# First feed-forward: 512-column products with added halves, and half of the modulation tiles on GpSimd and ScalarE

## The chip, the core and the metric

The kernel runs on one core of one Trainium2 chip, as one program. The metric is the device time of the program in microseconds (us). A core has five engines with a queue of instructions each, which run side by side and wait for each other by semaphores: TensorE (PE in the rows, PEld for its weight loads), VectorE (DVE), ScalarE (ACT), GpSimd (POOL) and SyncE (SP), which issues most transfers. An engine works through its queue in order.

## What is computed

Two layers of a decoder trunk on 256 positions of 1024 channels. Each layer has a mixer (layer 0: a state-space group beside attention; layer 1: a convolution module) and a gated feed-forward, both in front of a residual addition. Shift, scale and gate of each come from a modulation vector, the product of a condition vector with a large matrix. Cut to what matters here:

```python
def conv_ffn(h, w_up, w_gate, dw_w, dw_b, w_down):
    g = causal_dwconv(h @ w_gate, dw_w, dw_b)            # width 3 along the positions
    return (jax.nn.silu(g) * (h @ w_up)) @ w_down        # hidden width 2816

cs = jax.nn.silu(c)
for layer in range(2):
    mod = cs @ mod_w[layer] + mod_b[layer]               # 1024 x 6144
    sh1, sc1, g1, sh2, sc2, g2 = jnp.split(mod, 6, axis=-1)
    h = modulate(rms_norm(x, norm_g[layer, 0]), sh1, sc1)
    x = x + g1[:, None, :] * mixer(h)
    h = modulate(rms_norm(x, norm_g[layer, 1]), sh2, sc2)
    x = x + g2[:, None, :] * conv_ffn(h, ffn_w_up[layer], ffn_w_gate[layer], ..., ffn_w_down[layer])
return rms_norm(x, final_g)
```

## The kernel before

Everything is kept transposed: channels on the 128 partitions, the 256 positions (`T`) along a row. Weights come from memory in chunks of 128 x 1024 numbers (512 KB), one transfer each, in the fixed order of `chunk_order`, into 14 buffers (`raw0` to `raw9`, and four halves of `ABT0` and `ABT1`).

**Split products.** For accuracy each weight chunk is split in two: ScalarE writes a rounded copy `hi` (tiles `whi`, `whim`), VectorE the rest `lo = raw - hi` (tiles `wlo`, `wlom`). There are six such pairs of tiles, and a pair is free again when TensorE is through with its chunk (`release`). The activations `h` are split in the same way into a high and a low half of a row. A product of a 128 x 128 weight tile is then made of three parts, hi x high, hi x low and lo x high. `tile_mm` does it in three products of 256 columns into one result of 256 columns. `tile_wide` does the two with `hi` as one product of 512 columns, so that the result is two halves that have still to be added, and the third as a product of 256 columns.

**The feed-forward.** `ffn` goes through 44 chunks, gate and up in turn for 22 hidden blocks; the first three are done ahead in `ffn_lead`, so `run_seq` does 41 chunks of eight 128 x 128 tiles each, 328 tile steps. Its zone is called `b-` in layer 0 and `i-` in layer 1. In layer 0 the steps go by `tile_mm`, in layer 1 by `tile_wide`, and `post` has the additions of the halves for layer 1 alone. After each chunk `post` runs on ScalarE and VectorE: for a gate the width-3 convolution (`gate_tail`, tile `ac`), for an up chunk the product with the silu of the gate (tile `uu`) and its split into `hv` (`up_tail`). Then 22 chunks `down` are multiplied with `hv`, 22 steps for each of the 8 blocks of output; the last step of the first block needs the last `hv`.

**Modulation tiles.** 32 chunks `md` of the modulation matrix (four vectors of eight tiles, list `MD`) are mixed into the order of layer 0's feed-forward and eight (`MD1`) into that of layer 1. VectorE works each off in one instruction (`mod_dve`): the chunk times the condition vector `cb`, with its row sum into `modv`. The result of the product (`junk`) isn't used. After the eighth tile of a vector the bias is added.

**What sets the order.** The instructions are recorded in a `Plan`, which puts them in an order of its own for each engine (`arrange`): it goes through them by time as its cost formulas see it and takes the one with the highest rank among those that are ready, where the table `BONUS` adds a number to the rank of each group of instructions. The order is fixed when the kernel is built. All recorded instructions have the same line in the profile, 487 (of `getattr(getattr(self.nc, eng), fn)(*a, **k)`), so rows are told apart by their tiles.

Of the kernel before, what the change touches and what calls it, by code (L numbers as in the profile page):

```python
# [548 lines left out]
class Emit:  # L549
    def __init__(self, ctx, tc, nc, d, order):  # L550
        self.tc, self.nc, self.d, self.order = tc, nc, d, order
        self.pool = ctx.enter_context(tc.tile_pool(name="base", bufs=1))
        self.psp = ctx.enter_context(tc.tile_pool(name="psum", bufs=1, space=bass.MemoryType.PSUM))
        banks = [self.psp.tile([128, 512], F32, name=f"bank{i}") for i in range(8)]
        self.mm, self.aux = banks[:4], banks[4:]
        self.i_mm = self.i_aux = 0
        t = self.pool.tile
        self.raw_free = [t([128, 1024], F32, name=f"raw{i}") for i in range(RAW_BUFS)]
        self.split_free = [(t([128, 1024], F32R, name=f"whi{i}"), t([128, 1024], F32R, name=f"wlo{i}"))
                           for i in range(SPLIT_BUFS)]  # L560
# [89 lines left out]

    def mod_dve(self, c):
        _, l, s, f = c
        col = self.modv[l][:, s * 8 + f:s * 8 + f + 1]
        self.nc.vector.scalar_tensor_tensor(self.junk, self.raw[c], 1.0, self.cb, op0=OP.mult, op1=OP.mult,
                                            accum_out=col)
        self.done(c)
        if f == 7:
            mc = self.modcols(l, s)
            self.nc.vector.tensor_tensor(mc, mc, self.par("modb", l * 48 + s * 8, 8), op=OP.add)

    def low(self, n):
# [1419 lines left out]
```

## Time and profile before

| | us |
|---|---|
| median of 3 runs | 650.72 |
| lowest and highest | 647.98, 651.05 |
| the profiled execution | 652.09 |
| its span, first to last instruction | 650.3 |
| mixer of layer 0 and lead, up to the first step of zone `b-` | 0 to 164.2 |
| 41 chunks gate and up, layer 0 | 164.2 to 281.1 |
| down, layer 0 | 281.1 to 343.7 |
| convolution module, lead of layer 1 | 343.7 to 463.8 |
| 41 chunks gate and up, layer 1 | 463.8 to 579.0 |
| down, layer 1, and the end | 579.0 to 650.3 |

The rows below are of the profiled execution; the two microseconds between it and its span lie ahead of the first instruction and behind the last. A row of the timeline has the start, the duration, the engine, the operation, what it writes and reads, and its shape; consecutive instructions of one kind are merged with their count. A tile `bank` lies in the matmul's result memory (PSUM), all others in the on-chip main memory (SBUF). An instruction's duration overlaps a little with the next one's, so that the time an instruction costs its engine in a dense stretch is the distance from its start to the next start, its step.

### The profile page before, as it was taken

Reading aid. Unit: us, or ns where it says so; the run is one execution under the profiler, and the core shown is the slowest. Engines: PE = TensorE matmul, PEld = TensorE weight load, DVE = VectorE, ACT = ScalarE, POOL = GpSimd, SP = SyncE. Lnnn points to the kernel's source line nnn. Section 1 sums busy time; section 2 is a strip of 40 time slices with the busy share of each in tenths; the row PEclk is TensorE's granted clock in tenths of the full one; section 3 lists DMA queues with packets and bytes.
Section 4 is the critical chain, followed back from the end, with each engine's and each line's share of the span. In section 5 each row is a group of like instructions: output and inputs, shape, how many; then the busy total and the mean of one; then the engine's idle time right before and its main releaser. Section 6 shows DMA issues by size and latency. Waiting matters only on the chain.

```text
span 650.3 us, 13240 instructions
## 1 busy us (share of the span) xinstructions
PE 640.4 (98%) x5128; PEld 562.5 (87%) x5128; DVE 538.8 (83%) x1059; ACT 404.9 (62%) x736; POOL 41.2 (6%) x99
## 2 busy tenths in 40 slices
PE   8999999999999999999999999999999999999995
PEld 5789876899999999998899987568988888888885
DVE  8698996389999999999657999559999998997641
ACT  3479528897966666654446843377687766675431
POOL 4830000000000000000000222000000000000000
PEclk9999999999999999999999999999999999999998
DMA  8996888765489999999662798496476668764001
GB/s 325 405 377 224 291 324 300 316 217 210 134 288 320 325 331 303 338 328 365 195 196 81 245 325 245 154 380 263 135 280 199 201 214 259 217 210 164 1 0 66
DMA packets 45702, 158.50 MB, mean 244 GB/s; under 512 B 5535, under 2 KB 7112, under 8 KB 45640
## 3 DMA queue, kind: packets, MB, share of 16 engines
q1 hardware_dynamic: 43912, 153.84, 67.6%
q0 software_dynamic: 1152, 3.49, 1.9%
q8 instruction: 40, 0.66, 0.4%
q10 hardware_dynamic: 576, 0.33, 0.2%
q14 instruction: 22, 0.18, 0.1%
HBM read 153.10 MB, written 1.06 MB: 237 GB/s over the span
## 4 chain that ended last, share of the span: by engine, by line
PE 88%; DVE 7%; ACT 2%; DMA 1%; issue 1%; DVEq 0%; SPq 0%
PE bank L487 88%; DVE arena L487 4%; DVE wlo L487 1%; DMA raw<-w_in 1%; ACT CA L487 1%; DVE CS L487 1%; DVE U L487 1%; ACT whi L487 0%; ACT ABT L487 0%; DVE gp L487 0%; DVE nm L487 0%; DVE junk L487 0%; DVE h L487 0%; DVEq L2044 0%; DVE nt L487 0%
## 5 line engine op out<-in xcount | busy, mean ns | idle before, releaser
L487 PE MATMUL bank<-h,whi 128*128 128x256 f32 (+2 forms) x960 | 202.3, 303 | 0.2
L487 PEld LDWEIGHTS bank<-h,whi 128*128 128x128 f32 x960 | 152.4, 189 | 8.7 <-issue 1.0
L487 PE MATMUL bank<-h,wlo 128*128 128x256 f32 (+1 forms) x560 | 155.5, 283 | 0.0
L487 PE MATMUL bank<-h,whim 128*128 128x256 f32 (+1 forms) x664 | 149.1, 311 | 0.0
L487 PE MATMUL bank<-h,wlom 128*128 128x256 f32 x416 | 116.4, 281 | 0.0
L487 PEld LDWEIGHTS bank<-h,whim 128*128 128x128 f32 x664 | 108.2, 189 | 7.7
L487 PEld LDWEIGHTS bank<-h,wlo 128*128 128x128 f32 x560 | 104.5, 189 | 1.3 <-DVE CS L487 0.8
L487 DVE TENSOR_TENSOR wlo<-raw,whi 128x1024 fp32r<-128x1024 f32 x69 | 84.1, 1222 | 13.6 <-ACT whi L487 10.4
L487 ACT ACTIVATE whi<-raw 128x1024 fp32r<-128x1024 f32 x69 | 72.5, 1055 | 20.7 <-PE bank L487 13.7
L487 DVE TENSOR_TENSOR wlom<-raw,whim 128x1024 fp32r<-128x1024 f32 x60 | 72.9, 1222 | 10.5 <-ACT whim L487 10.3
L487 PEld LDWEIGHTS bank<-h,wlom 128*128 128x128 f32 x416 | 78.3, 188 | 0.1
L487 ACT ACTIVATE whim<-raw 128x1024 fp32r<-128x1024 f32 x60 | 62.6, 1054 | 22.7 <-PE bank L487 15.8
L487 PE MATMUL bank<-hv,whim 128*128 128x512 f32 (+1 forms) x236 | 67.7, 351 | 0.0
L487 PE MATMUL bank<-hv,whi 128*128 128x512 f32 x160 | 56.3, 393 | 0.0
L487 PE MATMUL bank<-hv,wlom 128*128 128x256 f32 x192 | 53.9, 281 | 0.0
L487 PEld LDWEIGHTS bank<-hv,whim 128*128 128x128 f32 x236 | 41.3, 189 | 6.2
L487 PE MATMUL bank<-hv,wlo 128*128 128x256 f32 x160 | 44.7, 279 | 0.0
L487 DVE SCALAR_TENSOR_TENSOR ac<-g,pp,ac 128x256 f32<-128x256 f32 x88 | 42.2, 482 | 2.5 <-ACT ac L487 0.8
L487 DVE SCALAR_TENSOR_TENSOR x<-bank,modv,x 128x256 f32<-128x256 f32 x54 | 25.6, 481 | 19.7 <-PE bank L487 19.1
L487 ACT ACTIVATE whi<-ABT 128x1024 fp32r<-128x1024 f32 x28 | 29.3, 1054 | 16.3 <-PE bank L487 15.3
L487 ACT ACTIVATE g<-bank 128x256 f32<-128x256 f32 x40 | 15.3, 382 | 36.4 <-PE bank L487 36.3
L487 PEld LDWEIGHTS bank<-hv,wlom 128*128 128x128 f32 x192 | 36.4, 190 | 0.0
(220 smaller groups left out, 1071.6 us busy)
## 6 DMA issues: line engine op xcount, KB each, us to landing
raw<-w_in SPq DMA_DIRECT2D x213, 512.0 KB, 5.3
ABT<-w_in SPq DMA_DIRECT2D x71, 512.0 KB, 4.9
a<-ap POOLq DMA_DIRECT2D x24, 142.0 KB, 5.4
x<-x_in SPq DMA_DIRECT2D x4, 256.0 KB, 4.2
arena<-scr SPq DMA_DIRECT2D x1, 1024.0 KB, 6.0
cb<-c_in SPq DMA_DIRECT2D x2, 512.0 KB, 4.9
kT<-bc_in SPq DMA_DIRECT2D x1, 512.0 KB, 11.4
out<-junk SPq DMA_DIRECT2D x2, 256.0 KB, 2.0
```

The costliest lines, as they stand in the source:

```text
L487: getattr(getattr(self.nc, eng), fn)(*a, **k)
```

## The change

`run_seq` gets `wide=("gate", "up")` in both layers, so layer 0's 328 steps become one product of 512 and one of 256 columns each, instead of three of 256. `post` then adds the two halves in layer 0 too: for a gate ScalarE copies the first half out of the bank (as it did) and VectorE adds the second half of the bank to it; for an up chunk ScalarE copies the second half out (new) and VectorE adds the first (new); the convolution and the product then read that sum from SBUF and no longer from the bank. Modulation tiles are numbered, and every second one goes to `mod_pool`: GpSimd multiplies the chunk by `cb` in place, then ScalarE copies it onto itself with a row sum into `modv`. The other tiles stay on VectorE. The list of numbers `BONUS` is another one throughout.

```diff
+ON_POOL = (1, 0)
...
-BONUS = {'a-evac': 335.5, 'a-gate_tail': -31, 'a-h_u': 30.1, 'a-lead': 1098.9,
...
+BONUS = {'a-evac': 602.1, 'a-gate_tail': 184.4, 'a-h_u': 1.4, 'a-lead': 2.7,
...
+        self.i_mod = 0
...
-                (self.mod_dve if c[0] == "md" else self.split)(c)
+                (self.mod if c[0] == "md" else self.split)(c)
...
+    def mod(self, c):
+        self.i_mod += 1
+        (self.mod_pool if ON_POOL[self.i_mod % len(ON_POOL)] else self.mod_dve)(c)
+        if c[3] == 7:
+            self.mod_bias(*c[1:3])
+
+    def mod_pool(self, c):
+        _, l, s, f = c
+        w = self.raw[c]
+        self.nc.gpsimd.tensor_tensor(w, w, self.cb, op=OP.mult)
+        self.nc.scalar.activation(w, w, AF.Copy, accum_out=self.modv[l][:, s * 8 + f:s * 8 + f + 1])
+        self.done(c)
+
+    def mod_bias(self, l, s):
+        mc = self.modcols(l, s)
+        self.nc.vector.tensor_tensor(mc, mc, self.par("modb", l * 48 + s * 8, 8), op=OP.add)
...
-        if f == 7:
-            mc = self.modcols(l, s)
-            self.nc.vector.tensor_tensor(mc, mc, self.par("modb", l * 48 + s * 8, 8), op=OP.add)
...
             if t == "gate":
                 nc.scalar.activation(g[:, 2:], ps[:, 0:T], AF.Copy)
-                if l == 1:
-                    ps = g[:, 2:]
-                    v.tensor_tensor(ps, psw[:, T:2 * T], ps, op=OP.add)
+                ps = g[:, 2:]
+                v.tensor_tensor(ps, psw[:, T:2 * T], ps, op=OP.add)
                 self.gate_tail(l, i, ps)
             else:
-                if l == 1:
-                    nc.scalar.activation(u, ps[:, T:2 * T], AF.Copy)
-                    v.tensor_tensor(u, ps[:, 0:T], u, op=OP.add)
-                    ps = u
+                nc.scalar.activation(u, ps[:, T:2 * T], AF.Copy)
+                v.tensor_tensor(u, ps[:, 0:T], u, op=OP.add)
+                ps = u
                 nc.scalar.activation(a, a, AF.Silu)
                 v.tensor_tensor(u, ps, a, op=OP.mult)
                 self.up_tail(i)
...
-        self.run_seq(ffn_seq(l)[3:], self.h, post, mids=mids, wide=("gate", "up") if l == 1 else ())
+        self.run_seq(ffn_seq(l)[3:], self.h, post, mids=mids, wide=("gate", "up"))
```

How the queues move is seen in the order of the instructions as built. On VectorE, in the middle of layer 0's gate and up chunks, stands before (`wlo...` is a split, `junk_1648,modv` a modulation tile, `ac` the convolution, `uu` and `hv` the product and its split):

```order
L487 SCALAR_TENSOR_TENSOR junk_1648,modv1_91<-raw3_72,cb_1649 128x1024
L487 SCALAR_TENSOR_TENSOR ac_0_1643<-g0_0_1641,pp_89,ac_0_1643 128x256 x2
L487 TENSOR_TENSOR wlo1_82<-raw9_78,whi1_81 128x1024
L487 TENSOR_TENSOR uu_0_1645<-bank1_62,ac_0_1643 128x256
L487 SCALAR_TENSOR_TENSOR junk_1648,modv1_91<-raw4_73,cb_1649 128x1024
L487 TENSOR_TENSOR hv_1640<-uu_0_1645,hv_1640 128x256
L487 TENSOR_TENSOR wlo2_84<-raw8_77,whi2_83 128x1024
L487 SCALAR_TENSOR_TENSOR junk_1648,modv1_91<-ABT0_87,cb_1649 128x1024
```

and at the like place now (`g0` from a bank is the added half of a gate, `uu` from a bank that of an up chunk):

```order
L488 TENSOR_TENSOR g0_1_1642<-bank2_63,g0_1_1642 128x256
L488 TENSOR_TENSOR wlo2_84<-raw8_77,whi2_83 128x1024
L488 SCALAR_TENSOR_TENSOR ac_1_1644<-g0_1_1642,pp_89,ac_1_1644 128x256 x2
L488 TENSOR_TENSOR uu_1_1646<-bank3_64,uu_1_1646 128x256
L488 TENSOR_TENSOR uu_1_1646<-uu_1_1646,ac_1_1644 128x256
L488 TENSOR_TENSOR wlo1_82<-raw9_78,whi1_81 128x1024
L488 TENSOR_TENSOR hv_1640<-uu_1_1646,hv_1640 128x256
L488 TENSOR_TENSOR wlo0_80<-ABT1_88,whi0_79 128x1024
```

Two additions have come in for each pair of chunks, and fewer modulation tiles stand between: from the first split of zone `b-` to the last `hv` VectorE has 24 of them before and 9 now, with 44 and 43 splits.

On ScalarE, at the same place, stands before (`whi...` is the other half of a split):

```order
L487 ACTIVATE hv_1640<-uu_1_1646 128x256
L487 ACTIVATE g0_0_1641<-bank0_61 128x256
L487 ACTIVATE ac_0_1643<-bank0_61,pp_89 128x256
L487 ACTIVATE whi0_79<-ABT1_88 128x1024
L487 ACTIVATE ac_0_1643<-ac_0_1643 128x256
L487 ACTIVATE whim0_1631<-raw3_72 128x1024
L487 ACTIVATE hv_1640<-uu_0_1645 128x256
```

and now:

```order
L488 ACTIVATE ac_0_1643<-g0_0_1641,pp_89 128x256
L488 ACTIVATE uu_0_1645<-bank1_62 128x256
L488 ACTIVATE whim0_1631<-raw0_69 128x1024
L488 ACTIVATE ac_0_1643<-ac_0_1643 128x256
L488 ACTIVATE hv_1640<-uu_0_1645 128x256
L488 ACTIVATE g0_1_1642<-bank2_63 128x256
L488 ACTIVATE whim1_1633<-ABT0_87 128x1024
L488 ACTIVATE raw7_76,modv1_91<-raw7_76 128x1024
L488 ACTIVATE uu_1_1646<-bank3_64 128x256
```

The copy of an up chunk's half and the row sums of GpSimd's tiles (`raw7_76,modv1_91`) have come into this queue; a row sum waits for GpSimd, and the next splits stand behind it. Of the 16 tiles that GpSimd takes in layer 0, 14 have their sum ahead of the last `hv`; four more stand in layer 1.

## Rows read from the trace of the kernel before

**Rows 1.** The page's first part: span, then busy time, share and instructions.

```profile
span 650.3 us, 13240 instructions
PE 640.4 (98%) x5128; PEld 562.5 (87%) x5128; DVE 538.8 (83%) x1059; ACT 404.9 (62%) x736; POOL 41.2 (6%) x99
```

**Rows 2.** The chain that ended last, in order of time: start, us, what.

```profile
91.24 328.39 PE bank L487 x2956
...
463.78 179.15 PE bank L487 x1051
```

**Rows 3.** Who waited for whom, TensorE only: total us, times, longest.

```profile
PE bank L487 <- DVE mrow L487: 1.7, 1, 1.7
PE bank L487 <- DMA raw<-w_in: 0.8, 1, 0.8
```

**Rows 4.** Stretches: length, then busy us (instructions) by engine, clock, DMA share, GB/s.

```profile
164.16:281.13 116.97, 116.97 (x987) 116.93 (x986) 115.91 (x195) 78.94 (x139) 0.00 (x0) 1.00 0.85 292
171.26:283.90 112.64, 112.64 (x944) 112.28 (x943) 111.58 (x181) 74.61 (x127) 0.00 (x0) 1.00 0.89 307
463.78:579.00 115.22, 115.22 (x656) 100.64 (x657) 108.06 (x192) 86.17 (x159) 0.00 (x0) 1.00 0.66 211
```

**Rows 5.** VectorE's timeline in the gate and up chunks: start, us, engine, operation.

```profile
217.71 1.23 DVE L487 TENSOR_TENSOR wlo<-ABT,whi 128x1024 fp32r<-128x1024 f32 x1
218.85 0.42 DVE L487 TENSOR_TENSOR uu<-bank,ac 128x256 f32<-128x256 f32 x1
219.18 1.22 DVE L487 SCALAR_TENSOR_TENSOR junk<-raw,cb 128x1024 f32<-128x1024 f32 x1
...
220.32 0.42 DVE L487 TENSOR_TENSOR hv<-uu,hv 128x256 fp32r<-128x256 f32 x1
220.66 1.22 DVE L487 TENSOR_TENSOR wlom<-raw,whim 128x1024 fp32r<-128x1024 f32 x1
```

**Rows 6.** Groups of the whole program by form: count, busy us, mean ns, idle before.

```profile
L487 ACT ACTIVATE whi<-raw 128x1024 fp32r<-128x1024 f32 x69 | 72.5, 1055 | 20.7 <-PE bank L487 13.7 <-DMA raw<-w_in 3.9 <-DMA ABT<-w_in 1.8
...
L487 DVE TENSOR_TENSOR uu<-bank,uu 128x256 f32<-128x256 f32 x21 | 8.7, 419 | 0.4 <-ACT uu L487 0.2
...
L487 DVE TENSOR_TENSOR g<-bank,g 128x256 f32<-128x256 f32 x20 | 8.4, 421 | 0.7 <-ACT g L487 0.4
...
L487 ACT ACTIVATE uu<-bank 128x256 f32<-128x256 f32 x21 | 7.7, 373 | 3.9 <-PE bank L487 2.5 <-DVE hv L487 1.2
...
L487 ACT ACTIVATION_READ_ACCUMULATOR CS<-CS,U 128x1 f32 x16 | 3.0, 189 | 0.0
```

**Rows 7.** Timeline of all engines, 37 to 39 us, one tile copied by GpSimd.

```profile
37.48 1.11 POOL L487 COPY D<-arena 128x1024 f32<-128x1024 f32 x1
...
37.80 0.81 DVE L487 SCALAR_TENSOR_TENSOR gp<-modv,gneg 128x1 f32<-128x1 f32 x1
```

**Rows 8.** VectorE's timeline at 43 us: the same instruction again.

```profile
42.96 0.16 DVE L487 SCALAR_TENSOR_TENSOR gp<-modv,gneg 128x1 f32<-128x1 f32 x1
```

**Rows 9.** Timeline at 74 us: GpSimd's other copy, and VectorE beside it.

```profile
73.85 1.10 POOL L487 COPY arena<-arena 128x1024 f32<-128x1024 f32 x1 [35.08 <-DMA arena<-scr]
73.97 1.88 DVE L487 TENSOR_TENSOR arena<-bank,CS 128x512 f32<-128x512 f32 x3
```

**Rows 10.** Timeline of GpSimd (first and last) and VectorE, 26 to 35 us.

```profile
26.66 0.25 POOL L487 TENSOR_SCALAR arena<-arena 128x16 f32<-128x16 f32 x1
...
33.51 1.24 DVE L487 TENSOR_TENSOR wlo<-raw,whi 128x1024 fp32r<-128x1024 f32 x1
...
33.65 1.17 POOL L487 TENSOR_SCALAR arena<-arena 128x16 f32<-128x16 f32 x1
```

**Rows 11.** VectorE's timeline at the last `hv`.

```profile
283.47 0.42 DVE L487 TENSOR_TENSOR hv<-uu,hv 128x256 fp32r<-128x256 f32 x1
```

**Rows 12.** TensorE's timeline: first step of down, and the last of its first block.

```profile
281.13 0.39 PE L487 MATMUL bank<-hv,whi 128*128 128x512 f32 x1
...
288.43 0.39 PE L487 MATMUL bank<-hv,whim 128*128 128x512 f32 x1
```

**Rows 13.** Stretch 100 to 125 us, columns as in rows 4.

```profile
100.00:125.00 25.00, 25.00 (x412) 18.61 (x403) 11.22 (x32) 20.52 (x57) 0.00 (x0) 0.93 0.99 381
```

More of the change, by code (lines that the diff above doesn't have):

```diff
@@ new lines @@
+BONUS = {'a-evac': 602.1, 'a-gate_tail': 184.4, 'a-h_u': 1.4, 'a-lead': 2.7, 'a-mod_dve': -53.3, 'a-modulate': 50.2, 'a-norm_r': -13.4, 'a-norm_y': 875.9, 'a-post': -145.9, 'a-pump': 11.6, 'a-split_hi': -107, 'a-up_tail': 518.5, 'ab0': 2.8, 'ab1': 257.9, 'abt0': -346.1, 'abt1': 3.6, 'b': 1059.7, 'b-gate_tail': 3.5, 'b-low': -179.6, 'b-mod_dve': -1352.4, 'b-mod_pool': -705.4, 'b-pump': 52.9, 'b-split_hi': -15.1, 'b-up_tail': 8, 'c-conformer': 695, 'c-low': 484.9, 'c-mod_bias': 4.8, 'c-mod_pool': 124.9, 'c-norm_gain': 594.1, 'c-pump': 310.4, 'c-raw_h': -54.6, 'c-residual': 166.2, 'c-shift_cols': 1.2, 'c-split_hi': -35.3, 'c-stat_acc': -8.1, 'c-stat_sq': -6.4, 'c-warm': -18.8, 'ca0': -469.2, 'ca1': -254.8, 'clear0': -87, 'clear1': 298.3, 'clear2': 110.4, 'clear3': 158.6, 'clear4': -14.6, 'cond': 18.8, 'cond0': -174.3, 'cond1': -1.3, 'cond2': 1.3, 'd-first': -1.2, 'd-h_u': 146.7, 'd-lead': -83.9, 'd-lead_evac': 2.3, 'd-modulate': 244, 'd-norm_r': 663.2, 'd-norm_y': -317.3, 'd-pump': 616.8, 'd-split_hi': 71.7, 'd-tap': 32.2, 'drive0': 746.9, 'drive1': 281.5, 'e-conformer': 3, 'e-conv_get': 241.7, 'e-conv_pe': 19.1, 'e-first': 1.3, 'e-last': -169, 'e-post': -6.4, 'e-pump': 29.7, 'e-split_hi': -135.6, 'e-warm': -34.1, 'exp1': -456.9, 'exp3': -68.6, 'f-centre': -7.5, 'f-conv_pe': -9.6, 'f-stat_sq': 34.5, 'feat1': -81.2, 'feat2': 352.3, 'feat3': 7.8, 'feat4': 150.4, 'feat5': 317.7, 'feat6': 8.7, 'feat7': 616.2, 'fin0': 112.9, 'fin1': 238.4, 'fin2': 248.7, 'fin3': 975.1, 'g-conformer': 61.7, 'g-ffn_open': 4.3, 'g-h_u': 1.4, 'g-low': 1.1, 'g-mod_evac': -221.9, 'g-mod_sel': -3.7, 'g-norm_r': -10.8, 'g-norm_y': 6.5, 'g-pump': 1.1, 'g-raw_h': -2.9, 'g-residual': -3.7, 'g-silu': -16.7, 'g-split_hi': -1.7, 'g-stat_acc': -1.7, 'g-stat_sq': 136, 'g-warm': -41.8, 'gelu': 1306.4, 'glub0forbin': -32.2, 'gneg': 914.4, 'h-evac': 401.4, 'h-gate_tail': 23, 'h-h_u': 55, 'h-lead': -519.7, 'h-low': 11.1, 'h-modulate': 926.6, 'h-norm_r': -241, 'h-norm_y': 13, 'h-post': 92.2, 'h-pump': -627.9, 'h-split_hi': 45.5, 'h-up_tail': 198.8, 'i-low': 7.1, 'i-mod_dve': -7, 'i-mod_pool': -745.1, 'i-post': 622.4, 'i-pump': 191.6, 'i-split_hi': -8.2, 'i-up_tail': 125.5, 'j-ffn': 270.4, 'j-finish': -846.7, 'j-low': -1.7, 'j-norm_y': 8.9, 'j-pump': 1.1, 'j-residual': 222.7, 'j-split_hi': -362.5, 'j-stat_acc': -408.4, 'j-stat_sq': -301.3, 'j-warm': 73.4, 'k_evac0': -16.7, 'k_evac1': -476.4, 'k_evac2': 5.8, 'k_evac3': -58.3, 'kd': 3.8, 'loada000': 8500, 'loada001': 8400, 'loada010': 8200, 'loada011': 8100, 'loada020': 7900, 'loada021': 7800, 'loada030': 7600, 'loada031': 7500, 'loada040': 7200, 'loada041': 7100, 'loada050': 6900, 'loada051': 6800, 'loada060': 6600, 'loada061': 6500, 'loada070': 6300, 'loada071': 6200, 'loadabo1': -125.1, 'loadabo2': -330.3, 'loadabo3': -25.6, 'loadabo4': -94.2, 'loadabo5': 607.3, 'loadabo6': 420, 'loadabo7': -19.1, 'loadbc': 7300, 'loadc': 9500, 'loadglu0': 38.3, 'loadglu1': 749.4, 'loadid': 9499, 'loadk0': 38.8, 'loadk1': 1.5, 'loadk2': 675.1, 'loadk3': -265.7, 'loadmp02': -2.2, 'loadmp03': 39.5, 'loadmp13': -48, 'loadmp14': -9.3, 'loadpp': 8600, 'loadpp2': -809.9, 'loadsel': 9498, 'loaduq0': 8300, 'loaduq1': 8000, 'loaduq2': 7700, 'loaduq3': 7400, 'loaduq4': 7000, 'loaduq5': 6700, 'loaduq6': 6400, 'loaduq7': 6100, 'loadv0': 6.5, 'loadv1': -9.7, 'loadv2': -110.6, 'loadv3': 2.7, 'loadx0': 9000, 'loadx1': 8900, 'loadx2': 8800, 'loadx3': 8700, 'main0': -4.4, 'main1': -2.5, 'main2': -257.2, 'main3': -193.3, 'main4': -349.8, 'main6': -988, 'main7': 33.1, 'mod_evac': 21.9, 'mod_pe004': -35.9, 'mod_pe048': 665.8, 'mod_pe1': -97.4, 'mod_pe2': 194.4, 'mod_sel': -443.7, 'mods0': 139, 'mods1': 1010.6, 'mods2': 174.1, 'mods3': -28.4, 'mods4': -91.1, 'mods5': -64.4, 'mods7': -515.6, 'norm': 443.8, 'norm0': 146.9, 'norm1': -28, 'norm2': 43.4, 'norm3': 565.3, 'out0': 6.8, 'out1': 5.2, 'out2': -1.4, 'out3': 444.1, 'poles': -1057.4, 'proj_k2': -1.1, 'proj_k3': 984.3, 'proj_o4firstrue': -2102.4, 'proj_o5': 642.2, 'proj_v0': -240.6, 'proj_v1': 246.1, 'proj_v2': -6.1, 'proj_v3': 15.1, 'q_evac': -285, 'rel': 1004.7, 'rel_table': 12.2, 'res1': -8.5, 'res2': 692.5, 'res3': -231, 'res4': -646.1, 'rot1': -37.3, 'score1': 668.9, 'score2': 969.7, 'score3': -20.4, 'set': 347.5, 'skip': 272.6, 'splitabo4': -29.8, 'splitabo5': 3.6, 'splitabo7': -3.1, 'splitglu0': -1929.1, 'splitglu1': -311.5, 'splitk1': 72.4, 'splitk2': 129.2, 'splitk3': -141.7, 'splitv0': -412, 'splitv1': -83.6, 'splitv2': 165.9, 'sq0': -52.4, 'sq1': 13.8, 'sq2': 471.5, 'sq3': 343.1, 'state': -557.5, 'turn0': 11.2, 'turn1': 45.9, 'turn2': 4.1, 'turn3': -2.4, 'u201': -75.6, 'u_evac': -830.4, 'vevac': 3.3, 'y0': -11, 'y1': -2.6, 'y2': -460.4, 'y3': -1.8}
```

1 line of the change is left out of this document (removed).

## The prediction

> **What bounds the kernel now.** I read the page's first part first: of a span of 650.3 us TensorE is busy for 640.4 [rows 1]. A busy TensorE alone proves little, since its instructions overlap, so I looked for what it waits for. The chain that ended last is TensorE without a break from 91 to 420 us and again from 464 us almost to the end [rows 2], and all waits that the profile puts down to TensorE's products come to 2.5 us [rows 3]. So TensorE bounds nearly every stage, and a change is worth what it takes off TensorE's own work, as long as the others keep up. The second question is how near the others are to not keeping up. In the stretch of the first feed-forward's gate and up chunks VectorE is busy for 111.58 of 112.64 us [rows 4]: it has no room, though today nobody waits for it, because part of that work is modulation tiles that nobody needs yet. ScalarE has 38 us to spare there, and GpSimd does nothing at all.
>
> **TensorE: minus 1.7 us.** What 328 steps cost in either form needs no guess, since the second feed-forward already has the new form with the same shapes. The stretch of 328 old steps is 116.97 us, that of 328 new ones 115.22, both at full clock (1.00, that is 2.4 GHz) and without a gap [rows 4]; 0.3566 against 0.3513 us a step. The columns are the same, 768 a step; only the number of instructions falls, and TensorE hides nearly all of what one costs. So the gain is 1.75 us, 0.3%, and it is all that this part can bring.
>
> **VectorE, without GpSimd's effect on it: about even.** I take the stretch from the first split of zone `b-` to the last `hv`, 112.6 us [rows 4]. By steps from start to start, a split costs 1.14 us, a short instruction 0.33 and a modulation tile 1.14 [rows 5]; with the read of its sum, where that doesn't overlap, I take 1.17. The new order has 15 modulation tiles less in the stretch: minus 17.6 us. It has 41 additions more; they are the two kinds that the second feed-forward shows at 419 and 421 ns [rows 6], like the short instructions of rows 5, so 0.335 a step: plus 13.7. One split less and three convolution instructions more come to plus 0.3. That makes 112.6 - 17.6 + 13.7 + 0.3 = 109.0 us, against 112.6 - 1.7 = 110.9 that TensorE leaves. VectorE would just keep up, with 1.9 us to spare.
>
> **VectorE beside GpSimd: about 25 us.** This is the term that decides. Nowhere in the trace does GpSimd multiply two tiles of 128x1024 beside VectorE, but it copies one of that size twice. During the first copy (37.48 to 38.59) VectorE issues a tiny instruction with two inputs from SBUF and takes 0.81 us over it, to within 0.02 us of the copy's end [rows 7]; the same instruction takes 0.16 us five microseconds later, with GpSimd idle [rows 8]. During the second copy VectorE runs three instructions of 512 numbers with one input from a bank in 1.88 us, 0.63 each, and isn't held up [rows 9]: 1024 numbers take 1.14 in rows 5. The other way round, a GpSimd instruction of 0.25 us takes 1.17 when VectorE runs a split, which reads two tiles from SBUF; it ends 0.07 us after the split [rows 10]. So the two engines exclude each other when VectorE reads two tiles from SBUF, for the whole instruction of the one that came first. In this stretch that is nearly everything that VectorE does: splits, modulation tiles, convolution, `hv`, and after the change the product `uu` too; only the 41 additions read a bank.
>
> How long does GpSimd's product hold VectorE up? From below by the copy, 1.1 us with one input; from above by twice that, 2.2, if the second input costs as much as the first. It does read twice as much, so I take 1.9, and 1.8 after what VectorE can still do meanwhile (1.0 and 2.1 at the ends). A tile then costs VectorE more in GpSimd's queue than the 1.17 us in its own. With 14 such tiles ahead of the last `hv`: 14 x 1.8 = 25.2 us (14.0 to 29.4).
>
> The Trainium skill has this as a rule. "SBUF — State Buffer", section "Who interferes with whom", says that a VectorE instruction with two SBUF inputs and a GpSimd instruction that reads SBUF take an exclusive lock, and that the later one waits for the whole of the other; rows 7 to 10 agree. "GPSIMD Engine Reference", section 3.1, gives 4497 ns for a `tensor_tensor` of 2048 numbers a row. As an estimate half of it is 2.25 us here; 14 x 2.15 would make 30.1 us in place of 25.2, and the time 672.7.
>
> **What of that reaches the end.** VectorE's 1.9 us of room take the first part. The last `hv` is written at 283.89 [rows 11] and needed by the last step of down's first block, which starts at 288.43 [rows 12]: 4.5 us more. The rest has no cover: a late `hv` stops TensorE in that block, and before that late additions hold the four banks and late splits starve the products; after it TensorE has lost the time for good. 25.2 - 1.9 - 4.5 = 18.8 us. Behind it, down has fewer VectorE instructions for each chunk, and layer 1's four GpSimd tiles fall into a stretch where VectorE has 115.22 - 108.06 = 7.2 us of room [rows 4]; moving them adds 4 x (1.8 - 1.17) = 2.5. Both at nothing; without that room the second would cost 2.5.
>
> **ScalarE.** 21 copies of 0.373, 14 sums of 1.055 and 0.189 [rows 6] add 25.2 us to its 74.6 [rows 4]: 99.8 of 110.9. It isn't the bound, but each sum waits for GpSimd, and the next splits are queued behind it, which VectorE and then TensorE wait for. Six pairs of split tiles are the cover. I put it at nothing, and at up to 4 us on the upper end.
>
> **The new order elsewhere** changes no work. TensorE has 2.5 us of waits to lose and can gain new ones; I take 0, with 2 us either way.
>
> **Sum.** -1.7 + 18.8 = +17.1 us on the profiled execution's 652.1. That is 1.4 above the median, so I count from the median: 650.7 + 17.1 = 667.8, say **668**. The ends are 14.0 - 6.4 - 1.7 = +5.9, 656.6 (655 with the order), and 29.4 - 6.4 - 1.7 + 4 = +25.3, 676.
>
> **Rivals.** *GpSimd waits instead, or the overlap is harmless.* If GpSimd's product yields to VectorE, each product ends up to 1.2 us later [rows 10]. The price is then ScalarE's: 14 x 1.2 = 17 us on 99.8, 6 us more than TensorE leaves, spread over 40 chunks and covered by the splits done ahead. VectorE's even balance holds and only TensorE's gain remains: 650.7 - 1.7 = 649.0, up to 651. For it speaks that each GpSimd row beside a split was the one that waited; against it row 7's 0.81. Chance 0.18.
>
> *A short hold-up.* If a product holds VectorE for about 0.7 us only (the wait in rows 7), 14 x 0.7 - 6.4 - 1.7 = +1.7, 652 to 655; beyond 0.8 us a tile the change is slower by over 0.5%. Against it: that wait began late in the copy and lasted to its end. Chance 0.06, split between the same and slower.
>
> *Faster by over 0.5%.* TensorE's gain isn't enough for it. In 100 to 125 us the clock's mean is 0.93 [rows 13], in a stretch of 412 mostly small products; 7% of 25 us is 1.75. If the new order keeps the clock up there and GpSimd does no harm, 650.7 - 1.75 - 1.75 = 647.2. It decides only if VectorE loses under half a microsecond a tile. Chance 0.04.
>
> That the change doesn't do what it says is ruled out by the order as built: the additions and 16 + 4 GpSimd products are there.
>
> **How the numbers follow.** Exclusion with VectorE held up has 0.72, 655 to 676, around 668. The short hold-up adds 0.06, the harmless overlap 0.18, faster 0.04. Slower by over 0.5% (3.25 us, about what a measurement of this kernel can tell from no change): 0.72 + 0.04 = 0.76. Within 0.5%: 0.20; faster: 0.04. The range from 650 to 676 takes in most of the first, the short hold-up and half of the harmless case.
>
> **What the next profile would show.** If this is right: the stretch of 328 steps takes some 130 us or more instead of 115, with TensorE waiting for VectorE's tiles `hv`, `g`, `uu` or `wlo`; splits of 1.22 us stand beside some of 2 to 3 us, each under a GpSimd product; products of 1.9 us or more on GpSimd; the second feed-forward's stretch is still about 115 us. It is wrong if VectorE's splits keep their 1.22 us beside GpSimd's products, if these take far under 1.5 us, or if TensorE's stretch is 115 us after all; a fall of the clock while TensorE waits would make it worse than I say.

## The result, and the profile after

The changed kernel takes 677.4 us (median; 676.2 to 681.0), against 650.8 for the kernel before (648.0 to 651.1; with one more execution than in the table ahead): ratio 1.043, 95% interval 1.038 to 1.048. So it is slower, as forecast and by the mechanism forecast, but by 26.6 us, not 17.1; the time lies 1.4 us above the range's upper end. The profiled execution after took 676.5 us with a span of 674.7; the spans differ by 24.4 us. (The profiled execution of before lay 1.3 us above its median, that of after 0.9 below.) The working below comes to 24.1 of the 24.4.

The page's first lines, to be held against [rows 1]: span, then busy time, share and instructions.

```profile
span 674.7 us, 12645 instructions
PE 645.7 (96%) x4800; PEld 548.3 (81%) x4800; DVE 565.5 (84%) x1060; ACT 428.6 (64%) x797; POOL 99.1 (15%) x119
```

TensorE issues 328 instructions less and yet is busy for longer, and it now waits. Who waited for whom, TensorE only, in the stretch of 164 to 306 us (total us, times, longest); before, this stretch had no such wait at all, and the whole program the two of [rows 3] and little else:

```profile
PE bank L488 <- DVE wlo L488: 5.6, 2, 4.0
PE bank L488 <- DVE wlom L488: 5.0, 3, 2.2
PE bank L488 <- DVE h L488: 2.1, 2, 1.7
PE bank L488 <- DVE uu L488: 1.6, 1, 1.6
PE bank L488 <- ACT whi L488: 1.5, 1, 1.5
PE bank L488 <- ACT whim L488: 1.1, 1, 1.1
PE bank L488 <- ACT fcol L488: 0.3, 1, 0.3
```

Four of the seven name VectorE's tiles, and they are 14.3 of the 17.2 us. Stretches of the changed kernel (columns as in [rows 4]): the first feed-forward's gate and up, its down, what lies between, the second gate and up.

```profile
167.47:305.38 137.91, 120.78 (x660) 102.69 (x659) 134.34 (x198) 96.00 (x182) 34.56 (x13) 0.98 0.67 231
305.38:369.07 63.69, 62.95 (x387) 56.03 (x386) 54.71 (x76) 34.07 (x50) 5.61 (x3) 1.00 0.82 294
369.07:487.20 118.13, 117.98 (x1102) 97.01 (x1100) 96.80 (x216) 69.14 (x129) 13.65 (x28) 1.00 0.68 246
487.20:603.45 116.25, 116.01 (x658) 100.53 (x658) 111.27 (x187) 87.67 (x164) 11.19 (x4) 1.00 0.64 220
```

The first row answers to the first of [rows 4]: VectorE is again busy nearly throughout, though it issues hardly more instructions than before (198 against 195). GpSimd's groups by form, count, busy us, mean ns, idle before:

```profile
L488 POOL TENSOR_TENSOR raw<-raw,cb 128x1024 f32<-128x1024 f32 x15 | 41.8, 2791 | 167.5 <-DMA raw<-w_in 144.0 <-ACT cb L488 23.5
...
L488 POOL TENSOR_TENSOR ABT<-ABT,cb 128x1024 f32<-128x1024 f32 x5 | 12.7, 2531 | 48.5 <-ACT uu L488 26.5 <-DMA ABT<-w_in 22.0
```

A product that has nothing to wait for takes 2.40 us (the one at 519.94); longer ones waited for VectorE first. What each does to VectorE shows best at 293 us. VectorE's timeline of the changed kernel (start, us, engine, operation):

```profile
293.54 0.43 DVE L488 TENSOR_TENSOR uu<-uu,ac 128x256 f32<-128x256 f32 x1
293.88 3.38 DVE L488 TENSOR_TENSOR wlo<-raw,whi 128x1024 fp32r<-128x1024 f32 x1
297.18 0.41 DVE L488 TENSOR_TENSOR hv<-uu,hv 128x256 fp32r<-128x256 f32 x1
297.52 1.21 DVE L488 TENSOR_TENSOR wlo<-ABT,whi 128x1024 fp32r<-128x1024 f32 x1
```

GpSimd's timeline beside it:

```profile
293.82 2.35 POOL L488 TENSOR_TENSOR raw<-raw,cb 128x1024 f32<-128x1024 f32 x1 [7.98 <-DMA raw<-w_in]
```

And TensorE's, which needs that `wlo`:

```profile
292.76 0.50 PE L488 MATMUL bank<-h,whi 128*128 128x512 f32 x1 [1.49 <-ACT whi L488]
297.31 0.58 PE L488 MATMUL bank<-h,wlo 128*128 128x256 f32 x1 [4.05 <-DVE wlo L488]
297.69 0.63 PE L488 MATMUL bank<-h,whi 128*128 128x512 f32 x1
298.12 0.41 PE L488 MATMUL bank<-h,wlo 128*128 128x256 f32 x1
```

The product began 0.06 us ahead of the split; the split took 3.38 us in place of 1.22 [rows 5], and TensorE stood still for it. (2.16 of its 4.05 us of waiting are this hold; for the rest VectorE was late already when it began the split.) All 20 products have such a neighbour on VectorE, a split, a modulation tile, `hv`, `h`, the product `uu`, a convolution step or (once) the bias sum: 1.05 to 3.46 us. Their excess, what they take beyond a like instruction with GpSimd idle, is 1.97 us on average. The one kind of instruction that is never held reads a bank: the additions, 82 in the program, keep the mean of [rows 6].

```profile
L488 DVE TENSOR_TENSOR uu<-bank,uu 128x256 f32<-128x256 f32 x42 | 17.5, 418 | 1.9 <-ACT uu L488 1.8
L488 DVE TENSOR_TENSOR g<-bank,g 128x256 f32<-128x256 f32 x40 | 16.7, 418 | 1.5 <-ACT g L488 1.5
```

### The profile page after: what moved, and what is told of

The parts are those of the page before. It is cut to its first block, busy times and chain, and to the rows that moved or that the text cites. A ratio compares the mean times of both kernels' runs of the same rounds, so it can differ in the third digit from the quotient of the medians.

```text
span 674.7 us, 12645 instructions
## 1 busy us (share of the span) xinstructions
PE 645.7 (96%) x4800; PEld 548.3 (81%) x4800; DVE 565.5 (84%) x1060; ACT 428.6 (64%) x797; POOL 99.1 (15%) x119
## 4 chain that ended last, share of the span: by engine, by line
PE 76%; DVE 14%; ACT 4%; DMA 4%; issue 2%; POOL 0%; DVEq 0%; SPq 0%; ACTq 0%
PE bank L488 76%; DMA raw<-w_in 3%; DVE wlom L488 2%; DVE wlo L488 2%; DVE ac L488 2%; DVE hv L488 1%; DVE arena L488 1%; DVE uu L488 1%; ACT whi L488 1%; ACT whim L488 1%; DVE junk L488 1%; DVE h L488 1%; ACT ac L488 1%; DVE g L488 1%; DMA ABT<-w_in 1%
## 5 line engine op out<-in xcount | busy, mean ns | idle before, releaser
L488 PE MATMUL bank<-h,whim 128*128 128x512 f32 (+1 forms) x496 | 148.5, 361 | 5.1 <-DVE h L488 2.1
L488 PEld LDWEIGHTS bank<-h,whi 128*128 128x128 f32 x800 | 134.7, 191 | 19.5 <-issue 2.2
L488 PEld LDWEIGHTS bank<-h,whim 128*128 128x128 f32 x496 | 88.0, 189 | 21.5 <-DVE h L488 2.7
L488 DVE TENSOR_TENSOR wlo<-raw,whi 128x1024 fp32r<-128x1024 f32 x69 | 85.9, 1250 | 10.7 <-ACT whi L488 10.6
L488 DVE TENSOR_TENSOR wlom<-raw,whim 128x1024 fp32r<-128x1024 f32 x60 | 78.6, 1319 | 9.8 <-ACT whim L488 9.8
L488 POOL TENSOR_TENSOR raw<-raw,cb 128x1024 f32<-128x1024 f32 x15 | 41.8, 2791 | 167.5 <-DMA raw<-w_in 144.0
L488 DVE SCALAR_TENSOR_TENSOR ac<-g,pp,ac 128x256 f32<-128x256 f32 x88 | 48.1, 551 | 1.1 <-ACT ac L488 0.2
L488 ACT ACTIVATE whi<-ABT 128x1024 fp32r<-128x1024 f32 x28 | 29.3, 1052 | 14.5 <-PE bank L488 12.2
L488 ACT ACTIVATE ac<-ac 128x256 f32<-128x256 f32 x44 | 18.2, 415 | 31.2 <-DVE ac L488 30.5
```

## The experiments

Both kernels and the twelve runs in one table. The stretches run between the same instructions of TensorE in each: start of the first feed-forward's first step by itself, its gate and up up to the first step of down, down, what lies between, the second gate and up (us; before, the first step is taken 0.25 us earlier than in [rows 4]). The ratio is to the kernel before, measured again beside each group of runs (medians of 649.5 to 650.8), with its 95% interval; the stretches are those of one profiled execution each.

| kernel | median | ratio | first step | gate, up | down | between | gate, up 2 |
|---|---|---|---|---|---|---|---|
| before | 650.8 | | 163.9 | 117.2 | 62.6 | 120.1 | 115.2 |
| changed | 677.4 | 1.043 (1.038 to 1.048) | 167.5 | 137.9 | 63.7 | 118.1 | 116.3 |
| e1 | 667.9 | 1.027 (1.024 to 1.030) | 169.1 | 130.2 | 62.6 | 118.2 | 115.3 |
| e2 | 681.0 | 1.049 (1.044 to 1.053) | 170.1 | 139.7 | 62.6 | 118.1 | 116.0 |
| e3 | 660.5 | 1.016 (1.012 to 1.020) | 170.0 | 118.2 | 66.5 | 118.4 | 115.3 |
| e4 | 662.9 | 1.019 (1.016 to 1.023) | 169.5 | 118.7 | 68.6 | 118.6 | 115.3 |
| e5 | 652.7 | 1.004 (1.002 to 1.007) | 167.6 | 115.9 | 62.7 | 118.2 | 115.2 |
| e6 | 653.5 | 1.007 (1.004 to 1.009) | 168.2 | 116.0 | 62.7 | 118.1 | 115.2 |
| e7 | 660.5 | 1.017 (1.014 to 1.019) | 169.4 | 121.8 | 63.0 | 118.1 | 115.3 |
| e8 | 670.9 | 1.032 (1.028 to 1.037) | 167.3 | 131.1 | 63.2 | 118.1 | 116.3 |
| e9 | 664.9 | 1.022 (1.019 to 1.025) | 169.2 | 122.1 | 66.8 | 118.1 | 115.6 |
| e10 | 657.0 | 1.011 (1.008 to 1.015) | 167.1 | 121.7 | 62.7 | 118.1 | 115.3 |
| e11 | 650.7 | 1.001 (0.999 to 1.003) | 163.8 | 116.8 | 63.6 | 118.4 | 115.3 |
| e12 | 649.1 | 1.000 (0.997 to 1.002) | 161.8 | 117.2 | 62.6 | 118.2 | 115.3 |

The theory (A): GpSimd's product keeps VectorE out, and TensorE then waits for VectorE. Rivals: ScalarE's sums, queued among the splits (B); the additions and the 512-column form (C); the new table of numbers (D).

### One part at a time, ordered anew

**e1, the wide products alone.**

```diff
-ON_POOL = (1, 0)
+ON_POOL = (0,)
```

> The changed kernel with every modulation tile back on VectorE and none on GpSimd; the 512-column products, the additions and the new table stay. Theory A (each GpSimd product of 128x1024 keeps VectorE out for 1.97 us, the mean excess of the 16 VectorE instructions that stood beside one): VectorE's ledger up to the last hv is 112.6 us with 8 modulation tiles less than before (the order now has 15 of them ahead of the last hv, 23 before) and 41 additions more, 112.6 - 9.4 + 13.7 = 117 us against 110.9 that TensorE leaves; 4.5 of the 6 us are covered, TensorE gains 1.75: about 651 us, and 651 to 655 with what the new table costs ahead of this stretch (3.5 us in the changed kernel's trace). Rival C (it is the additions and the 512-column form that overload VectorE, GpSimd hardly matters): 665 us or more.

Measured: 667.9 us, far off theory A's number and in C's range, but not for C's reason: VectorE is busy for only 117.90 of the 130.15 us of the stretch. At its worst place TensorE waits for a split of ScalarE's, and this one for a transfer. ScalarE's timeline of e1:

```profile
267.55 1.06 ACT L488 ACTIVATE whi<-raw 128x1024 fp32r<-128x1024 f32 x1 [6.98 <-DMA raw<-w_in]
```

Ahead of that (262.8 to 266.6) VectorE had worked off three modulation tiles. SyncE, which issues the transfers, waits for VectorE there (up to 5.0 us at a time from 250 to 270 us), so buffers come free late: a bad order. That it is bad because the table was made for a program with other instructions is argued, not shown.

**e2, the GpSimd products alone.**

```diff
-        self.run_seq(ffn_seq(l)[3:], self.h, post, mids=mids, wide=("gate", "up"))
+        self.run_seq(ffn_seq(l)[3:], self.h, post, mids=mids, wide=("gate", "up") if l == 1 else ())
```

(and the copies and additions of layer 0 go, as before the change)

> The changed kernel with the first feed-forward's products back in the old 256-column form without additions; every second modulation tile stays on GpSimd, the new table stays. Theory A: VectorE's ledger is 112.6 - 7 x 1.17 + 14 x 1.97 = 132 us against TensorE's 112.6: 19.4 us late, 4.5 covered, +15: about 666 us, 662 to 672 with the table, and VectorE instructions of 2.5 to 3.4 us beside each GpSimd product. Rival C (the additions overload VectorE): 651 to 655, since they are gone.

Measured: 681.0 us, 9 above theory A's upper end, and far from C's 655: with the old products and no addition the loss is all there. VectorE's excess beside GpSimd is 27.6 us. Of the 9 us, 2.6 are a start still later than the 3.5 us allowed for, and the mean clock of the stretch is 0.95; the rest isn't accounted for.

**e3, the product left out.**

```diff
-        self.nc.gpsimd.tensor_tensor(w, w, self.cb, op=OP.mult)
```

> The changed kernel without the GpSimd product: ScalarE still sums the tile, but unmultiplied, so that the modulation values of every second tile are left out of the computation. Everything else, ScalarE's 20 sums and the additions too, is as in the changed kernel. Theory A: VectorE's ledger is 109 us against 110.9, TensorE gains 1.75 and the new table may cost up to 3.5 ahead of the stretch: 649 to 653 us, and the stretch of the 328 steps takes about 115 us. Rival B (ScalarE's sums, queued among the splits, are what delays VectorE and TensorE): as long as the changed kernel without the waits for GpSimd, 665 to 677.

Measured: 660.5 us, between the two. The gate and up stretch is 118.2 us, as A says, so that B falls there; but the start is 6 us late and down 3.9 us longer than before.

**e4, the new table alone, on the kernel before.**

```diff
-BONUS = {'a-evac': 335.5, ...}
+BONUS = {'a-evac': 602.1, ...}
```

> The kernel before with the new table of numbers and nothing else. In the changed kernel's trace the first 512-column step comes 3.5 us later than the first step of that chunk before, ahead of any harm that GpSimd did; the stretch between the two feed-forwards is 1.9 us shorter. Theory D (that is the table's doing): 652 to 655 us, with the feed-forward's first step about 3.5 us later than before. Rival (it comes from the first two GpSimd products, which start at 164.4 us beside the last step of the norm): 650 to 652, and the feed-forward starts within 1 us of before.

Measured: 662.9 us. The start is 5.6 us late with no product on GpSimd, so that this is the table's doing; but down loses 6.0 us more, which the changed kernel doesn't. VectorE's timeline of e4 shows why:

```profile
293.88 1.22 DVE L487 SCALAR_TENSOR_TENSOR junk<-ABT,cb 128x1024 f32<-128x1024 f32 x1
...
296.16 1.22 DVE L487 SCALAR_TENSOR_TENSOR junk<-raw,cb 128x1024 f32<-128x1024 f32 x1
...
297.50 2.35 DVE L487 TENSOR_TENSOR wlom<-raw,whim 128x1024 fp32r<-128x1024 f32 x2
```

TensorE waits 4.18 us there (until 298.78) for the first of these two `wlom`, which comes behind modulation tiles. So the four runs settle little: who takes an instruction out of this program, or puts the table on another one, also changes the order of the rest, which is worth some 8 to 12 us (e3 against e5 below, e4 against before). The next six keep each engine's order exactly as in the changed kernel and change only what is issued in GpSimd's place.

### The same order, other instructions

The edit of these runs stands where the planned order is issued; the lines marked * differ:

```diff
             for eng, fn, a, k, _ in ops[i][2] if ops[i][1] == "bundle" else [ops[i]]:
+                if eng == "gpsimd" and len(a) > 2 and is_ap(a[2]) and a[2].tensor.name.startswith("cb"):
+                    continue          # *
                 getattr(getattr(self.nc, eng), fn)(*a, **k)
```

**e5, no product** (the * as above).

> The changed kernel with each engine's instructions in exactly its order, the 20 GpSimd products alone dropped where they would be issued, so that every second modulation tile is summed unmultiplied and those values are left out. (The run without the product before this one was ordered anew and came to 660.5 us, 17 below the changed kernel; its stretches were 118 and 66 us for the two halves of the feed-forward, its start 170 us.) Theory A (VectorE is held 27.3 us by the 14 products ahead of the last hv; 6.4 of that covered; the half-speed clock after TensorE's longest wait cost 2.8): 677.4 - 20.9 - 2.8 - 1.0 in the second feed-forward = 653 us, up to 660 where the order itself costs something at the lead and in down; the feed-forward's gate and up stretch at 115 to 119 us. Rival B (ScalarE's sums among the splits, or the order itself, carry the loss): 668 us or more.

Measured: 652.7 us. That settles the main question: with the additions, ScalarE's sums and the order all in place, dropping the 20 products alone takes the time from 677.4 to 652.7, 24.7 of the 26.6 us. C falls, and so do the sums' own time and place in the queue (B); whether their waits for GpSimd matter, e6 shows. The stretch of e5 (columns as above) has VectorE busy for 110.40 of 115.85 us, TensorE almost without gaps:

```profile
167.59:283.44 115.85, 115.61 (x660) 100.65 (x659) 110.40 (x200) 99.06 (x185) 0.00 (x0) 1.00 0.79 276
```

And all of TensorE's waits from 160 to 604 us:

```profile
PE bank L490 <- DVE h L490: 0.2, 1, 0.2
```

**e6, GpSimd writes only** (* is two `memset(a[0], 0.0)` and `continue`).

> As the run without the product in the same order, but in the product's place GpSimd writes the tile twice with zeros (two memsets of 128x1024), reading nothing; the modulation values of these tiles are left out of the computation. GpSimd is then busy for about 2 us a tile, as with the product's hold. If what keeps VectorE out is GpSimd reading SBUF: the time of the run without the product, 653 to 660 us, VectorE's splits 1.2 us throughout. If any GpSimd instruction on SBUF does it: 1.6 to 2 us a tile, 668 to 677 us, with splits of 2.5 to 3.4 us beside the memsets.

Measured: 653.5 us, the time of e5. GpSimd's timeline of e6:

```profile
185.91 0.96 POOL L489 MEMSET raw<- 128x1024 f32 x1 [18.17 <-DMA raw<-w_in]
186.92 0.95 POOL L490 MEMSET raw<- 128x1024 f32 x1
```

VectorE's beside it:

```profile
186.46 1.22 DVE L492 TENSOR_TENSOR wlom<-raw,whim 128x1024 fp32r<-128x1024 f32 x1
187.60 0.42 DVE L492 TENSOR_TENSOR hv<-uu,hv 128x256 fp32r<-128x256 f32 x1
```

A split with two SBUF inputs runs its 1.22 us beside a GpSimd that writes. It is GpSimd's reading that keeps VectorE out. ScalarE's sums wait for GpSimd for 3.3 us in e6 (164 to 306 us), longer than in the changed kernel (2.1), so that their waits aren't the cause either, and B is gone. ("SBUF — State Buffer", section "Who interferes with whom", in the Trainium skill says the same: such a VectorE instruction contends with a GpSimd instruction that reads SBUF, not with one that only writes it.)

**e7, half a product** (* is `a = [x[:, 0:512] for x in a]`).

> The changed kernel in its own order, each GpSimd product cut to its first 512 columns (the other half is summed unmultiplied: left out of the computation). Theory A (VectorE waits for the rest of the GpSimd instruction): a hold of about 1.0 us a tile, 14 x 1.0 - 6.4 = 7.6 instead of 20.9, and no or a shorter fall of the clock: 661 to 666 us, VectorE's excess beside each product 0.8 to 1.1 us. If instead a product costs VectorE a fixed fee whatever its length: 672 to 677 us.

Measured: 660.5 us, 7.9 above e5, a little under what was expected; layer 0's 16 products (one of which met no instruction that it could hold) held VectorE up for 13.1 us, the longest excess 1.11. The price goes with the size. A fixed fee falls.

**e8, four quarters** (* issues four products of 256 columns and `continue`).

> The changed kernel in its own order, each GpSimd product issued as four products of 256 columns; nothing is left out. Theory A with whole instructions (who comes first keeps the other out until its instruction ends): VectorE is held up to four times for 0.5 us instead of once for 2, and each quarter may wait for VectorE in turn: the same sum, 672 to 682 us, the longest single excess on VectorE below 0.7 us, ScalarE's sums later. If short GpSimd instructions slip in beside VectorE's reads of a bank or between its instructions: 660 to 670 us.

Measured: 670.9 us, between the two ranges named: 18.2 us above e5 instead of 24.7. VectorE's timeline of e8, where GpSimd works on four quarters from 186.53 to 190.98:

```profile
186.87 1.76 DVE L492 TENSOR_TENSOR wlom<-raw,whim 128x1024 fp32r<-128x1024 f32 x1
188.56 0.96 DVE L492 TENSOR_TENSOR hv<-uu,hv 128x256 fp32r<-128x256 f32 x1
189.44 0.41 DVE L492 TENSOR_TENSOR g<-bank,g 128x256 f32<-128x256 f32 x1
189.77 0.62 DVE L492 TENSOR_TENSOR uu<-uu,ac 128x256 f32<-128x256 f32 x1
190.31 1.75 DVE L492 TENSOR_TENSOR wlom<-raw,whim 128x1024 fp32r<-128x1024 f32 x1
```

The engines alternate: a split loses 0.54 us, `hv` 0.54, and no excess is over 0.58. Taken together VectorE loses 21.1 us instead of 31.5 (both from 160 to 345 us): between two quarters it gets a turn, and some quarters fall beside an addition from a bank, which isn't held.

**e9, the same tiles on VectorE** (* drops the product, and ScalarE's sum is replaced at its place by VectorE's `scalar_tensor_tensor(junk, w, 1.0, cb, mult, mult)` with the sum).

> The changed kernel in its own order, but each GpSimd product and the ScalarE sum behind it replaced by VectorE's own product with sum, issued where the sum stood; nothing is left out. It prices the same 14 tiles on VectorE instead of GpSimd. Theory A (1.17 us of VectorE a tile in its own queue against a hold of 1.95): 14 x 1.17 = 16.4 us on the 652.65 of the same order without products, about 6.5 to 7 of them covered: 660 to 664, faster than the changed kernel by 13 to 17 us. Rival (GpSimd did take load off VectorE, and the loss lay in one or two badly placed products): 677 us or more.

Measured: 664.9 us, 0.9 above what was expected, 12.5 below the changed kernel and 12.2 above e5. So VectorE loses less by doing a tile itself than by GpSimd doing it: the offload costs more than what it takes off.

**e10, a GpSimd instruction with one input** (* is `tensor_scalar(a[0], a[0], 1.0, None, op0=OP.mult)` and `continue`).

> The changed kernel in its own order, with GpSimd multiplying the tile by 1.0 in place (one input from SBUF) instead of by the second tile; those modulation values are left out. If one input is enough to keep VectorE out, for as long as the instruction lasts: about 1.1 us an instruction by the copies of that size before the change, a hold of 0.7 to 0.9 us, 14 x 0.8 - 7 = 4 on 652.65: 655 to 660 us, with VectorE's excess beside each. If it takes two inputs on GpSimd's side: 653 us and VectorE's instructions undisturbed, as with the memsets.

Measured: 657.0 us, 4.4 above e5, as expected, but the reason given for it is only half right. GpSimd's timeline of e10:

```profile
199.05 3.20 POOL L489 TENSOR_SCALAR raw<-raw 128x1024 f32<-128x1024 f32 x1 [11.64 <-DMA raw<-w_in]
```

VectorE's beside it:

```profile
199.53 1.26 DVE L491 SCALAR_TENSOR_TENSOR ac<-g,pp,ac 128x256 f32<-128x256 f32 x1
200.71 0.41 DVE L491 TENSOR_TENSOR uu<-bank,uu 128x256 f32<-128x256 f32 x1
201.04 0.47 DVE L491 SCALAR_TENSOR_TENSOR ac<-g,pp,ac 128x256 f32<-128x256 f32 x1
201.44 1.21 DVE L491 TENSOR_TENSOR wlom<-raw,whim 128x1024 fp32r<-128x1024 f32 x1
```

One input is enough to hold VectorE up (`ac` takes 1.26 us in place of 0.47), but this instruction takes 2.8 us alone, not 1.1, and holds VectorE for 0.8 of them: a second `ac` runs at full speed while it goes on until 202.25, and a split begins at full speed; another split ran its whole 1.22 us, from 185.87, inside such an instruction of 184.63 to 187.40.

### What the order costs, and whether any part pays

**e11, the old table ahead of the feed-forward, no product** (e5's edit, and the old numbers for every name but those of the zones `b-` to `j-`).

> The changed kernel without the GpSimd product (those values left out) and with the old table's numbers for the loads, the mixer and the lead, the new ones from the first feed-forward's zone on. It prices the new order ahead of the feed-forward, where the same order without products starts its first 512-column step 3.7 us later than the kernel before. If that is the table's doing: the start at 164 to 165 us and 648 to 650 us in all, 3 us below the 652.65. If it has another cause (the graph changed, a transfer): 652 to 653 and the start at 167 us or later.

Measured: the start is at 163.8 us, as before the change, so the 3.7 us are the table's doing. The whole is 650.7 us, ratio 1.001 (0.999 to 1.003), just above what was expected: 1 us is lost in down. Even with a product that cost nothing and an order without loss there would be no gain to measure.

**e12, the kernel before with the new numbers for the zones `d-` to `j-`.**

> The kernel before with the new numbers for the zones behind the first feed-forward only (conformer, second feed-forward, end). In all kernels with the new table the stretch between the two feed-forwards takes 118.1 us instead of 120.1. If that gain stands by itself: 1.9 us below the kernel before, 647.6 to 649 us. If it hung on what came before: no difference.

Measured: what lies between takes 118.2 us, 1.9 less than before, as expected; but the ratio, 0.9995 (0.997 to 1.002), can't tell it from no change. No run beats the kernel before.

## Why the prediction was right about the mechanism, and too low

By its own steps, in us of the profiled executions:

| step | forecast | measured |
|---|---|---|
| TensorE's gain from 512 columns | -1.75 | -1.4 (117.2 to 115.9, e5) |
| VectorE's balance without GpSimd's effect | even, 1.9 to spare | even (e5: no wait of TensorE for it over 0.2) |
| hold of VectorE ahead of the last `hv` | 14 x 1.8 = 25.2 | 15 x 1.95 = 29.3 |
| covered | 1.9 + 4.5 = 6.4 | 2.7 + 3.7 = 6.4 |
| ScalarE's sums | 0, up to 4 | 0 (e5, e6) |
| layer 1's four products | 0, 2.5 without room | +1.0 |
| new order elsewhere | 0, 2 either way | +1.6 (start +3.6, between -1.9) |
| TensorE's clock | not in the sum | nothing that shows |
| sum | +17.1 | -1.4 + 29.3 - 6.4 + 1.0 + 1.6 = +24.1, of 24.4 |

That is 7.0 more than forecast: 4.1 in the hold, 1.6 in the order, 1.0 in layer 1, 0.3 in TensorE's gain. (The medians differ by 2.2 us more than these two executions do; what that is no trace shows.)

**Right:** the gain from the form, VectorE's ledger, who holds whom, what the last `hv` covers, and that each tile costs VectorE more on GpSimd than in its own queue. That reading came from one row, the 0.81 us of [rows 7] against the 0.16 of [rows 8]. The signs named for the next profile are there: a stretch over 130 us, waits for VectorE's tiles, splits of 3 us under a product, products of 2.4 us.

**The step that failed: the hold, 14 x 1.8.** It is 15 x 1.95, 4.1 us more. The count went by the sums: 14 tiles have their sum on ScalarE ahead of the last `hv`. But what holds VectorE is the product, which comes before the sum. The fifteenth product begins at 307.40 and holds a convolution step (`ac`, 2.51 us in place of 0.48) ahead of the last `hv`; its sum begins only at 313.45. GpSimd, VectorE, ScalarE and TensorE of the changed kernel:

```profile
307.40 2.45 POOL L488 TENSOR_TENSOR raw<-raw,cb 128x1024 f32<-128x1024 f32 x1 [1.96 <-DMA raw<-w_in]
...
307.63 2.51 DVE L488 SCALAR_TENSOR_TENSOR ac<-g,pp,ac 128x256 f32<-128x256 f32 x1
...
313.20 0.42 DVE L488 TENSOR_TENSOR hv<-uu,hv 128x256 fp32r<-128x256 f32 x1
...
313.45 1.04 ACT L488 ACTIVATE raw<-raw 128x1024 f32<-128x1024 f32 x1
...
313.68 0.50 PE L488 MATMUL bank<-hv,whim 128*128 128x512 f32 x1 [0.74 <-DVE hv L488]
```

TensorE waits there for the last `hv`, as the prediction had it. The same two instructions in e5, where VectorE has the same order without a hold:

```profile
286.71 0.42 DVE L490 TENSOR_TENSOR hv<-uu,hv 128x256 fp32r<-128x256 f32 x1
...
290.87 0.39 PE L490 MATMUL bank<-hv,whim 128*128 128x512 f32 x1
```

From the first step (167.47 and 167.59) the last `hv` comes 26.6 us later than in e5, so VectorE made up 2.7 of the 29.3; in e5 it is written 3.7 us before it is needed (287.13 and 290.87). 26.6 - 3.7 = 22.9, and gate, up and down together grow by 23.0 us from e5 to the changed kernel.

The size was off too. The bounds were 1.0 and 2.1 and the value taken 1.8. The product takes 2.40 us alone, above the 2.2 that came from doubling a copy of 1.1 [rows 7]; e10's 2.8 us for one input show that a GpSimd instruction's time can't be had by counting inputs. The page "GPSIMD Engine Reference" of the Trainium skill (section 3.1) states 4497 ns for 2048 numbers; half of it, the prediction's estimate of 2.25, is nearer. The 30.1 us of hold that it gave lie near the measured 29.3 by luck: 2.15 a tile is too much, 14 tiles are too few.

**The upper end.** 676 has 4 us for ScalarE that never came, and leaves out the 2 us for the new order that the lower end has (656.6 to 655); with them it would have been 678.

**The clock fell, and nothing shows that it cost time.** The prediction named a fall of the clock as a thing that would make it worse, but gave it no number. In the changed kernel's row of 297 us TensorE came back from its longest wait, 4.05 us, at half speed. Stretches of the changed kernel, that wait and what followed:

```profile
292.76:297.31 4.55, 0.50 (x1) 0.19 (x1) 4.27 (x5) 4.03 (x8) 2.35 (x1) 0.85 0.48 142
297.31:302.31 5.00, 5.00 (x16) 4.32 (x17) 4.83 (x9) 3.07 (x6) 0.00 (x0) 0.50 0.74 249
```

The clock is 0.50 (1.2 GHz) up to 302.6 us. A step takes 0.64 us there (297.69 to 298.33) and 0.35 at full speed, so of these 5.3 us TensorE loses 2.4. But at 313.68 it waits for the last `hv` all the same, and VectorE wasn't kept waiting by the slower TensorE: from the split at 293.88 to the last `hv` it is idle for 0.30 us, between the same two instructions of e5 for 0.31. The changed kernel's stretch and e5's:

```profile
293.88:313.20 19.32, 15.62 (x75) 13.37 (x75) 19.02 (x20) 12.55 (x24) 7.43 (x3) 0.82 0.70 252
...
273.79:286.71 12.92, 12.92 (x76) 11.30 (x75) 12.61 (x22) 12.07 (x24) 0.00 (x0) 1.00 0.91 326
```

So e5's expectation, which gave 2.8 us to the clock and counted 14 holds, met 652.7 by luck. A wait of 2.24 us at 264.5 had no such sequel. The other executions of the changed kernel (676.2 to 681.0 us) have mean clocks of 0.985 to 0.978, this one 0.990; the longest has the lowest, but the shortest has 0.985.

**Too small, the order.** "0, 2 either way" was assumed, not read. In this pair of executions the two sides nearly meet (+1.6), but e4 and e11 show what the table alone can do at the start: 3.6 to 5.6 us. In all eleven kernels with the new table ahead of the feed-forward TensorE waits 1.2 to 2.8 us for `CS` near 90 us; with the old one (before, e11, e12) it doesn't. In eight of the eleven the clock's mean from 88 to 98 us is then 0.83; in the changed kernel, e5 and e10 waits of 1.2, 1.8 and 1.4 us leave it at 1.00. So part of it is the clock, and why it falls in one run and not in another stays open. A start also differs by itself: e12, with the old table there, begins at 161.8 and the kernel before at 163.9, with clocks of 1.00 and 0.86 from 110 to 122 us. What splits the 3.6 us of the changed kernel's own start was not tried; its waits there, 1.2 for `CS` and 1.0 for transfers, are the larger part.

**Layer 1's room** of 7.2 us [rows 4] was there, its four holds came to 7.9 us less the tiles that VectorE no longer did, and 1.0 us was lost all the same (without the holds, in e5 and e6, the stretch is at 115.2). That a hold of 2 us comes in one piece, which room spread over the stretch doesn't cover, is argued; the profile shows only a wait of 0.2 us for `g`.

The rivals: that GpSimd yields or the overlap does no harm is out (20 of 20 products held VectorE up), the short hold-up too; the gain through a kept clock didn't come: from 110 to 122 us its mean is 0.86, as before.

## What to carry to other kernels

An idle GpSimd is no free engine for elementwise work as long as VectorE is the tight one and reads two SBUF tiles: look in the trace for one small VectorE instruction beside a GpSimd one, and price the hold before moving work, and count the instructions that hold, not those that follow them. If work must go there, short instructions hold less than one long one (e8), and what only writes holds nothing (e6). When a program's order comes from a table, judge an edit with the order held fixed; otherwise the runs price the order.

## What the runs showed of the hardware that was not expected

- GpSimd's hold isn't simply the time that its instruction takes; it is longer for two inputs and for longer rows: up to 2.24 us for two inputs of 1024 numbers (2.40 us alone), 1.11 for two of 512, 0.58 for two of 256, 0.84 for one input of 1024 (2.8 us alone), nothing for a memset of 1024 (0.96). The Trainium skill ("SBUF — State Buffer", section "SBUF: two separate sides") has whoever comes first holding the other for the whole instruction; for two inputs these rows nearly agree, for e10's one input they don't: a split ran its 1.22 us inside it. What GpSimd does in the rest of that instruction no run here shows.
- GpSimd's multiplication of one tile by a constant takes longer (2.77 us) than its product of two tiles (2.40), and more than twice its copy of [rows 7].
- After a wait of 4.05 us TensorE ran at half speed for 5.3 us, after one of 2.24 us at full speed. The length of the wait doesn't settle it: after 1.4 us for `CS` the clock fell in e3, after 1.8 it didn't in e5.
